# Storing a matmul's moving rows as pairs of 64-byte pieces in the expert stages and the feed-forward

## The chip, the cores and the metric

The kernel runs on one core of a Trainium2 chip, in one launch. The metric is device microseconds from start to end of the program; three runs of the kernel before gave 1620.09, 1614.03 and 1619.76 us, median 1619.76. Durations below come from one profiled execution of it, which took 1614.73 us, with a span of 1612.8 us from the first to the last recorded instruction.

## The reference, cut to what matters

Two transformer blocks on 256 tokens of width 1024, in fp32. The first ends in an expert layer (PEER), the second in a gated feed-forward with a short convolution:

```python
def peer_ffn(xn, wq, subkeys, u_tab, v_tab):          # T = 256 tokens, D = 1024
    q = (xt @ wq).reshape(T, 8, 2, 128)
    s = jnp.einsum('thpd,hpnd->thpn', q, subkeys)     # 8 heads x 2 halves x 128 keys
    ...                                               # top 16 of 128 x 128 = 16384 experts
    hdn = gelu(einsum('cd,chkd->chk', xc, u_tab[ic])) * gates
    return einsum('chk,chkd->cd', hdn, v_tab[ic])

    # second block, feed-forward (D_FF = 2816)
    u = conv_general_dilated(h @ w_up, w_conv, ...) + b_conv
    val, gt = jnp.split(u, 2, axis=-1)
    x = x + gate_f * ((jax.nn.silu(gt) * val) @ w_down)
```

## The kernel before, in words

Activations are held transposed: features on the 128 partitions, the 256 tokens along each partition. A row of 256 tokens in fp32 is 1024 bytes, and such a row is the *moving* operand of nearly every matmul; a 128x128 block of weights is the *stationary* one, loaded by a weight load (PEld) of its own while the matmul before it runs.

Precision comes from splitting. Each 128x1024 tile of weights is brought by one DMA of 512 KB (`raw`, L292), rounded by ScalarE into `hi` (L304), and VectorE forms `lo` = raw - hi (L306). The activations are split likewise into `xh` and `xl`, or `Hh` and `Hl` (`split`, L363 and L364). `mm3` then runs three matmuls per block, all of type fp32r with 256 columns: `hi` with `xh` (L322), `hi` with `xl` (L323), and after these `lo` with `xh` (L325). One tile of weights is 8 blocks, so 24 matmuls.

Three stages use it as the change touches it.

- The expert layer's first half (from 330 us to 782 us). `xh` and `xl` hold the normed input as eight rows. The queries are 16 units (`route`, `t_unit`), all but the first as `mm3`; then `u_pair` takes the 16384 rows of `u`, not gathered but all of them, as 128 units of 24 matmuls. Between them run the routing (VectorE, ScalarE) and, from 550 us on, the gates, which scale the result by the few experts chosen (`choose`, `gate`, with fp16 matmuls L1263).
- The expert layer's second half (782 to 1151 us). For each of 128 row blocks of `v`, one 256-token row of the hidden tile is split into `Hh` and `Hl`, and `mm3` adds it to eight accumulators `acc` in PSUM. After every second block `self.step()` advances a background job, `ada` (L376 to L399), by one step: it reads one more tile of modulation weights (`raw`, the same ring of 4 buffers) and VectorE multiplies and adds it (L388). After 8 such tiles 8 transposes follow (L394), and the next group begins.
- The feed-forward (1426 to 1607 us): 44 units of `up` with `xh`, `xl`; the first runs unsplit (L457), the second is split inside `norm_apply` (L465). Then 22 row blocks of `down` with `Hh`, `Hl`, interleaved two steps behind.

The instructions of an engine run in the order that they are queued. Weight tiles rotate through 4 `raw` buffers and, in the expert stages, 2 pairs of `hi` and `lo`. SyncE issues all DMAs in the order of the program.

`shim` places a tile: it allocates a few bytes in a pool and so shifts what follows. With `AT_U`, `AT_V` and `AT_FF` at 192, the rows of all three stages begin 192 bytes past a multiple of 256, and the weight blocks (512 bytes each) begin at a multiple of 256. The other stages (first mixer, second mixer) have the same form of matmul and are not touched.

Of the kernel before, what the change touches and what calls it, by code (L numbers as in the profile page):

```python
# [6 lines left out]
F32 = mybir.dt.float32  # L7
F32R = mybir.dt.float32r
# [8 lines left out]
T = 256  # L17
# [19 lines left out]

AT_B1, AT_U, AT_V, AT_B2, AT_FF = 192, 192, 192, 192, 192

# [230 lines left out]
class Prog:  # L270
# [17 lines left out]


    def raw(self, u, n=1024):  # L290
        t = self.wp.tile([128, 1024], F32, name="raw", tag="raw")
        self.sy.dma_start(t[:, :n], self.a["w"][u, :, :n])  # L292
        return t
# [19 lines left out]
    def mm3(self, terms, whi, wlo, xhi, xlo, inner=False):  # L313


        if inner:
            for t in terms:
                self.mm3([t], whi, wlo, xhi, xlo)
            return
        m = self.pe.matmul  # L320
        for out, w, x, start, stop in terms:
            m(out, whi[w], xhi[x], start=start, stop=False, skip_group_check=True)  # L322
            m(out, whi[w], xlo[x], start=False, stop=False, skip_group_check=True)  # L323
        for out, w, x, start, stop in terms:
            m(out, wlo[w], xhi[x], start=False, stop=stop, skip_group_check=True)  # L325

# [34 lines left out]

    def split(self, src, hi, lo):
        self.s.activation(hi, src, AF.Copy)  # L363
        self.v.tensor_tensor(lo, src, hi.bitcast(F32), OP.subtract)  # L364
# [78 lines left out]
    def norm_apply(self, h, gname, sh, sc, xh, xl, raws, pool, tag):  # L443
# [3 lines left out]
        ps = [pool.tile([128, T], F32, name="mmo", tag=tag, bufs=2) for _ in range(2)]  # L447
        for d in range(8):
# [4 lines left out]
            if whole:  # L453
                x = self.sm.tile([128, T], F32, name="nx", tag="sq", bufs=2)
                s.activation(x, tmp, AF.Identity, bias=sh[:, d:d + 1])
                for i in whole:
                    self.pe.matmul(ps[i], raws[i][:, c], x, start=(d == 0), stop=(d == 7))  # L457
                self.split(x, xh[:, d], xl[:, d])
            else:
                s.activation(xh[:, d], tmp, AF.Identity, bias=sh[:, d:d + 1])  # L460
                v.scalar_tensor_tensor(xl[:, d], tmp, sh[:, d:d + 1], xh[:, d].bitcast(F32), OP.add, OP.subtract)
            for p in range(3):
                for i in range(2):
                    if i not in whole:
                        self.pe.matmul(ps[i], raws[i][p // 2][:, c], (xh, xl, xh)[p][:, d], start=(d + p == 0), stop=(d == 7 and p == 2), skip_group_check=True)  # L465
        return ps
# [600 lines left out]
    def peer(self):  # L1067
# [25 lines left out]
        h = self.h  # L1093
        xh = xp.tile([128, 8, T], F32R, name="xh")
        xl = xp.tile([128, 8, T], F32R, name="xl")
        first = self.norm_apply(h, "n2", self.mod1[:, 24:32], self.mod1[:, 32:40], xh, xl, self.raws, ps2, "x")
        self.dump("xn2", xh.bitcast(F32))

# [224 lines left out]
        for i in range(128):  # L1323
            hi, lo = self.wsplit(wu["v"] + i)
            Hh = vp.tile([128, T], F32R, name="Hh")
            Hl = vp.tile([128, T], F32R, name="Hl")
            self.split(hslice(i // 2 * 2)[:, i % 2], Hh, Hl)
# [386 lines left out]
    def ffn(self):  # L1714
# [4 lines left out]
        with ExitStack() as st:  # L1719
# [6 lines left out]
            self.shim(rp, AT_FF)  # L1726
            xh = bp.tile([128, 8, T], F32R, name="xh")
            xl = bp.tile([128, 8, T], F32R, name="xl")
            self.shim(bp, 256 - AT_FF)
# [7 lines left out]
            def up(i):  # L1737
# [11 lines left out]
                v.tensor_tensor(val, val, gt, OP.mult)  # L1749
                Hh = rp.tile([128, T], F32R, name="Hh", tag="Hh")  # L1750
                Hl = rp.tile([128, T], F32R, name="Hl", tag="Hl")
                if i == 0:
# [34 lines left out]
```

## Time and profile before

| | |
|---|---|
| three runs | 1620.09, 1614.03, 1619.76 us |
| the profiled execution | 1614.73 us, span 1612.8 us |
| TensorE busy (matmul) | 1563.8 us, 97% of the span, 13022 matmuls |
| TensorE weight loads busy | 1500.2 us, 93% |
| VectorE, ScalarE busy | 1264.7 us (78%), 1020.4 us (63%) |
| granted TensorE clock, mean | 0.995 |
| DMA | 303.42 MB read, mean 190 GB/s |

A recorded matmul lasts from its start to its modelled end and overlaps the next, so a duration of 276 ns does not mean that one starts every 276 ns. The view of the chain that ended last gives the part of each that nothing overlaps: eight matmuls there with 0.91 us are spaced by 0.91 / 8 = 0.114 us.

### The profile page before, as it was taken

The page shows a single profiled execution, that of the slowest core. Times are in us where ns is not written, and L with a number is a line of the kernel's source. Part 1 is how long each engine was busy: PE and PEld are TensorE (multiplying, and loading weights), DVE is VectorE, ACT ScalarE, POOL GpSimd, SP SyncE. Part 2 cuts the span into 40 slices and gives each one's busy share as a digit, 9 for nine tenths or more (in the row PEclk, how much of TensorE's full clock was granted, in tenths as well). Part 3 has the DMA queues.
Part 4 walks back from the last instruction along what each step waited for, and adds up shares of the span by engine and source line. Part 5 has one row for each costly group of instructions (what it writes and reads, how often), then busy time and mean ns, then how long its engine had stood idle before and what let it go on. Part 6 is the DMA issues. An engine that isn't in the chain of part 4 may idle for free.

```text
span 1612.8 us, 33487 instructions
## 1 busy us (share of the span) xinstructions
PE 1563.8 (97%) x13022; PEld 1500.2 (93%) x13022; DVE 1264.7 (78%) x2731; ACT 1020.4 (63%) x2093; POOL 6.6 (0%) x43
## 2 busy tenths in 40 slices
PE   6999999999999999999999999999999999999998
PEld 5888898989999999999999999999898998889998
DVE  7887887878788787788777777777798886777776
ACT  4575765555545799998544444444678877755553
POOL 0000000000000000000000000000000000000000
PEclk8999999999999999999999999999999999999999
DMA  8632346645544544444677877788657322435553
GB/s 303 250 105 92 119 129 226 233 141 178 188 163 171 178 167 167 164 164 170 216 265 263 273 257 261 258 281 270 202 200 252 131 96 93 153 131 196 191 191 116
DMA packets 85262, 306.64 MB, mean 190 GB/s; under 512 B 9456, under 2 KB 10992, under 8 KB 84976
## 3 DMA queue, kind: packets, MB, share of 16 engines
q1 hardware_dynamic: 85104, 304.51, 55.5%
q8 instruction: 102, 1.67, 0.4%
q14 instruction: 56, 0.46, 0.1%
HBM read 303.42 MB, written 1.05 MB: 189 GB/s over the span
## 4 chain that ended last, share of the span: by engine, by line
PE 79%; DVE 9%; DMA 6%; ACT 3%; issue 1%; SPq 0%; DVEq 0%; ACTq 0%
PE mmo L322 14%; PE mmo L325 14%; PE mmo L323 13%; PE acc L323 6%; PE acc L322 6%; DMA raw<-w 6%; PE acc L325 5%; DVE lo L306 3%; PE pg L1263 2%; ACT hi L304 1%; PE facc L325 1%; PE facc L322 1%; PE facc L323 1%; PE z L699 1%; DVE acc L388 1%
## 5 line engine op out<-in xcount | busy, mean ns | idle before, releaser
L304 ACT ACTIVATE hi<-raw 128x1024 fp32r<-128x1024 f32 (+1 forms) x465 | 490.6, 1058 | 374.7 <-PE acc L323 167.7
L306 DVE TENSOR_TENSOR lo<-raw,hi 128x1024 fp32r<-128x1024 f32 (+1 forms) x465 | 565.5, 1218 | 171.9 <-ACT hi L304 168.1
L322 PE MATMUL mmo<-xh,hi 128*128 128x256 f32 x2032 | 496.8, 285 | 1.4 <-ACT hi L304 0.4
L323 PE MATMUL mmo<-xl,hi 128*128 128x256 f32 x2032 | 488.3, 280 | 0.0
L322 PEld LDWEIGHTS mmo<-xh,hi 128*128 128x128 f32 x2032 | 382.6, 189 | 5.4 <-ACT hi L304 1.7
L323 PEld LDWEIGHTS mmo<-xl,hi 128*128 128x128 f32 x2032 | 382.8, 188 | 2.0 <-issue 0.2
L325 PE MATMUL mmo<-xh,lo 128*128 128x256 f32 x2032 | 282.0, 280 | 4.7 <-DVE lo L306 4.6
L325 PEld LDWEIGHTS mmo<-xh,lo 128*128 128x128 f32 x2032 | 254.5, 188 | 7.1 <-DVE lo L306 6.5
L323 PE MATMUL acc<-Hl,hi 128*128 128x256 f32 x1024 | 244.6, 281 | 3.5 <-DVE Hl L364 2.6
L322 PE MATMUL acc<-Hh,hi 128*128 128x256 f32 x1024 | 243.7, 278 | 1.1 <-ACT Hh L363 1.1
L323 PEld LDWEIGHTS acc<-Hl,hi 128*128 128x128 f32 x1024 | 192.5, 188 | 8.0 <-DVE Hl L364 7.5
L322 PEld LDWEIGHTS acc<-Hh,hi 128*128 128x128 f32 x1024 | 192.4, 188 | 1.3 <-ACT Hh L363 1.3
L325 PE MATMUL acc<-Hh,lo 128*128 128x256 f32 x1024 | 139.5, 278 | 0.0
L325 PEld LDWEIGHTS acc<-Hh,lo 128*128 128x128 f32 x1024 | 127.3, 188 | 0.0
L388 DVE SCALAR_TENSOR_TENSOR acc<-raw,sil,acc 128x1024 f32<-128x1024 f32 x70 | 89.8, 1283 | 44.2 <-DMA raw<-w 43.9
L1245 ACT ACTIVATE D<-iota,i 128x128 f16<-128x128 f16 x256 | 84.6, 404 | 0.2
L1252 DVE TENSOR_TENSOR B<-O,iT 128x512 f16<-128x512 f16 x128 | 46.1, 418 | 0.0
L322 PE MATMUL facc<-Hh,hi 128*128 128x256 f32 x176 | 41.3, 276 | 0.0
L323 PE MATMUL facc<-Hl,hi 128*128 128x256 f32 x176 | 41.3, 276 | 0.0
L364 DVE TENSOR_TENSOR Hl<-hidA,Hh 128x256 fp32r<-128x256 f32 x96 | 40.2, 418 | 0.0
L363 ACT ACTIVATE Hh<-hidA 128x256 fp32r<-128x256 f32 x96 | 38.3, 400 | 0.0
L1246 ACT ACTIVATE A<-D 128x512 f16<-128x512 f16 x64 | 37.8, 628 | 0.0
(503 smaller groups left out, 2269.7 us busy)
## 6 DMA issues: line engine op xcount, KB each, us to landing
raw<-w SPq DMA_DIRECT2D x542, 512.0 KB, 4.2
aw<-w SPq DMA_DIRECT2D x16, 512.0 KB, 7.3
raw<-w SPq DMA_DIRECT2D x6, 384.0 KB, 3.5
whole<-w SPq DMA_DIRECT2D x4, 512.0 KB, 7.0
c<-w SPq DMA_DIRECT2D x3, 512.0 KB, 6.5
x<-xT SPq DMA_DIRECT2D x2, 512.0 KB, 5.8
hres<-xT SPq DMA_DIRECT2D x1, 1024.0 KB, 5.4
sk<-w SPq DMA_DIRECT2D x2, 512.0 KB, 5.5
```

The costliest lines, as they stand in the source:

```text
L304: self.s.activation(hi[:, :n], r[:, :n], AF.Copy)
L306: self.v.tensor_tensor(lo[:, :n], r[:, :n], hi[:, :n].bitcast(F32), OP.subtract)
L322: m(out, whi[w], xhi[x], start=start, stop=False, skip_group_check=True)
L323: m(out, whi[w], xlo[x], start=False, stop=False, skip_group_check=True)
L325: m(out, wlo[w], xhi[x], start=False, stop=stop, skip_group_check=True)
L363: self.s.activation(hi, src, AF.Copy)
L364: self.v.tensor_tensor(lo, src, hi.bitcast(F32), OP.subtract)
L388: v.scalar_tensor_tensor(acc, w, sc, acc, OP.mult, OP.add)
L1245: s.activation(D[:, j], iota, AF.Abs, bias=i1[:, t0 + j:t0 + j + 1])
L1246: s.activation(A, D, AF.Relu, scale=-1.0, bias=1.0)
L1252: v.tensor_tensor(B[p], O, row(1 + p), OP.mult)
L1263: mm(pg[:, j], B[p][:, :, j], A[:, j], start=(j + p == 0), stop=(j == 3 and p == 1), skip_group_check=True)
```

## The change

Each 256-token row of the moving operands in these three stages is stored in another order. It is seen as 16 pieces of 16 tokens (64 bytes). Even pieces go into the first 512 bytes of the row, odd pieces into the second 512: piece 2j lies at byte 64 j, piece 2j + 1 at byte 512 + 64 j. A matmul reads them in token order, so its moving access pattern goes 64 bytes in the lower half, 64 bytes in the upper half, and so on; outputs and sums are the same numbers in the same order. In the second half of the expert layer (`back=True`) the pairs are stored from the end, so that the addresses of the pairs fall while they are read.

`like` gives a plain row the matching view, so that the instructions that write `xh`, `xl`, `Hh`, `Hl` scatter, and PSUM is written as before. `AT_U` and `AT_V` go from 192 to 128, which moves the rows of both expert stages by 64 bytes.

Queues of SyncE and TensorE hold the same instructions in the same order. ScalarE's and VectorE's hold the same too, but the writers of these rows now have the form 128x8x2x16 in place of 128x256. On GpSimd the memsets of the shims change size, and one falls away.

```diff
-AT_B1, AT_U, AT_V, AT_B2, AT_FF = 192, 192, 192, 192, 192
+AT_B1, AT_U, AT_V, AT_B2, AT_FF = 192, 128, 128, 192, 192
...
+    def paired(self, pool, k, name, back=False, **kw):
+        t = pool.tile([128, k, 2, 8, 16], F32R, name=name, **kw)
+        if back:
+            t = t[:, :, :, ::-1]
+        return t.rearrange("p k e j w -> p k j e w")
+
+    def like(self, x, y):
+        return x.rearrange("p (j e w) -> p j e w", e=2, w=16) if len(y.shape) == 4 else x
...
         for out, w, x, start, stop in terms:
+            out = self.like(out, xhi[x])
             m(out, whi[w], xhi[x], start=start, stop=False, skip_group_check=True)
             m(out, whi[w], xlo[x], start=False, stop=False, skip_group_check=True)
         for out, w, x, start, stop in terms:
-            m(out, wlo[w], xhi[x], start=False, stop=stop, skip_group_check=True)
+            m(self.like(out, xhi[x]), wlo[w], xhi[x], start=False, stop=stop, skip_group_check=True)
...
     def split(self, src, hi, lo):
+        src = self.like(src, hi)
         self.s.activation(hi, src, AF.Copy)
...
-        xh = xp.tile([128, 8, T], F32R, name="xh")
-        xl = xp.tile([128, 8, T], F32R, name="xl")
+        xh, xl = self.paired(xp, 8, "xh"), self.paired(xp, 8, "xl")
...
-            Hh = vp.tile([128, T], F32R, name="Hh")
-            Hl = vp.tile([128, T], F32R, name="Hl")
+            Hh, Hl = self.paired(vp, 1, "Hh", True)[:, 0], self.paired(vp, 1, "Hl", True)[:, 0]
...
-            xh = bp.tile([128, 8, T], F32R, name="xh")
-            xl = bp.tile([128, 8, T], F32R, name="xl")
+            xh, xl = self.paired(bp, 8, "xh"), self.paired(bp, 8, "xl")
...
-                Hh = rp.tile([128, T], F32R, name="Hh", tag="Hh")
-                Hl = rp.tile([128, T], F32R, name="Hl", tag="Hl")
+                Hh, Hl = self.paired(rp, 1, "Hh", tag="Hh")[:, 0], self.paired(rp, 1, "Hl", tag="Hl")[:, 0]
```

## Rows read from the trace of the kernel before

**Rows 1.** The page's first part: busy time of each engine, share of the span, number of instructions.

```profile
PE 1563.8 (97%) x13022; PEld 1500.2 (93%) x13022; DVE 1264.7 (78%) x2731; ACT 1020.4 (63%) x2093; POOL 6.6 (0%) x43
```

**Rows 2.** Busy time by stage: first half of the expert layer in two parts, second half, feed-forward. Columns: stretch in us and its length; PE, PEld, DVE, ACT, POOL busy us (instructions); granted clock, DMA share, GB/s.

```profile
400.00:600.00 200.00, 195.98 (x1720) 193.28 (x1719) 162.92 (x426) 135.27 (x257) 0.00 (x0) 1.00 0.51 174
600.00:781.00 181.00, 181.00 (x1748) 179.88 (x1747) 151.46 (x300) 161.87 (x414) 0.25 (x2) 1.00 0.47 164
783.00:1151.00 368.00, 364.52 (x3121) 359.99 (x3121) 271.97 (x346) 174.61 (x255) 0.65 (x7) 1.00 0.79 264
1426.00:1607.00 181.00, 180.51 (x1570) 179.76 (x1570) 135.52 (x207) 104.25 (x162) 0.00 (x0) 1.00 0.50 169
```

**Rows 3.** The chain that ended last from 429 to 460 us (the `u` units): start us, us, engine, tile, line, count.

```profile
430.97 0.91 PE mmo L325 x8
433.69 0.91 PE mmo L325 x8
436.41 0.91 PE mmo L325 x8
439.13 0.91 PE mmo L325 x8
440.04 0.44 PE psc L1127 x4
...
443.03 0.94 PE mmo L325 x8
...
445.86 0.94 PE mmo L325 x8
...
448.69 0.94 PE mmo L325 x8
```

**Rows 4.** Matmuls by form (count | busy us, mean ns of one | idle before), in 442 to 457 us, then in 400 to 781 us, 783 to 1151 us and 1426 to 1607 us.

```profile
L325 PE MATMUL mmo<-xh,lo 128*128 128x256 f32 x40 | 5.5, 281 | 0.0
...
L323 PE MATMUL mmo<-xl,hi 128*128 128x256 f32 x971 | 231.2, 279 | 0.0
...
L325 PE MATMUL acc<-Hh,lo 128*128 128x256 f32 x1022 | 138.9, 278 | 0.0
...
L325 PE MATMUL mmo<-xh,lo 128*128 128x256 f32 x336 | 45.0, 276 | 0.0
```

**Rows 5.** Two forms with 128 fp32 columns moving against 128 columns of weights, by tile: count, duration ns min/median/max, first and last start.

```profile
L394 PE MATMUL mmo<-c,acc x80: 270/272/328, 220.8 to 1145.9; 128*128 128x128 f32 x80
...
L908 PE MATMUL pr<-V,MQ x32: 272/275/347, 146.9 to 276.2; 128*128 128x128 f32 x32
```

**Rows 6.** The transposes that end a group of the background job, in order of time: start us, us of the whole row; and from the view by tile the stage's first matmul: count, duration ns min/median/max, first and last start.

```profile
833.73 1.04 PE L394 MATMUL mmo<-c,acc 128*128 128x128 f32 x8
...
885.32 1.03 PE L394 MATMUL mmo<-c,acc 128*128 128x128 f32 x8
...
936.88 1.04 PE L394 MATMUL mmo<-c,acc 128*128 128x128 f32 x8
...
L322 PE MATMUL acc<-Hh,hi x1024: 276/276/384, 782.5 to 1151.3; 128*128 128x256 f32 x171
```

**Rows 7.** The chain by line from 783 to 1151 us, from 784 to 833 us and from 886 to 937 us, the first pieces of the last, and two rows of matmuls by form in 784 to 833 us and 835 to 885 us.

```profile
by line: PE acc L323 26.8%; PE acc L322 24.8%; PE acc L325 24.1%; DMA raw<-w 14.7%; DVE acc L388 2.9%; DVE lo L306 2.5%; issue 1.4%; ACT hi L304 1.4%; DVE Hl L364 1.0%; PE mmo L394 0.7%; DVEq L388 0.1%; DVEq L306 0.0%; ACTq L304 0.0%
...
by line: PE acc L323 33.9%; PE acc L322 33.4%; PE acc L325 32.9%
...
by line: DMA raw<-w 34.8%; PE acc L323 17.2%; PE acc L325 16.2%; PE acc L322 16.0%; DVE acc L388 7.8%; DVE lo L306 4.8%; issue 3.0%; DVE Hl L364 0.7%; DVEq L388 0.2%
...
886.96 4.01 DMA raw<-w
891.06 1.30 DVE acc L388
892.37 4.64 DMA raw<-w
897.10 1.29 DVE acc L388
898.42 4.43 DMA raw<-w
902.94 1.29 DVE acc L388
...
L325 PE MATMUL acc<-Hh,lo 128*128 128x256 f32 x138 | 19.2, 281 | 0.0
...
L325 PE MATMUL acc<-Hh,lo 128*128 128x256 f32 x142 | 19.1, 277 | 0.0
```

**Rows 8.** The chain from 400 to 600 us and from 600 to 781 us, by line.

```profile
by line: PE mmo L325 24.1%; PE mmo L322 23.9%; PE mmo L323 23.3%; DVE lo L306 7.4%; DVE res L1187 4.5%; PE pg L1263 3.5%; PE psc L1127 2.2%; issue 1.9%; DVE eq L1186 1.6%; ACT hi L304 1.1%; DVE eq L1184 1.0%; DVE mr L1112 0.8%; DVE ti L1111
...
by line: PE mmo L322 29.7%; PE mmo L323 28.8%; PE mmo L325 28.6%; PE pg L1263 12.6%; ACT hi L304 0.5%; issue 0.0%
```

**Rows 9.** The splits of one hidden row in the second half, by tile: count, duration ns min/median/max.

```profile
L363 ACT ACTIVATE Hh<-hidA x96: 395/400/405, 782.0 to 1053.3; 128x256 fp32r<-128x256 f32 x96
L364 DVE TENSOR_TENSOR Hl<-hidA,Hh x96: 415/418/421, 782.7 to 1055.6; 128x256 fp32r<-128x256 f32 x96
```

**Rows 10.** Unsplit fp32 matmuls of 256 columns: four in a row in order of time (start us, us), and another form by tile (duration ns min/median/max).

```profile
1255.79 1.03 PE L616 MATMUL rp<-x,c 128*128 128x256 f32 x4
...
L703 PE MATMUL z<-x,whole x64: 377/379/774, 24.3 to 68.0; 128*128 128x256 f32 x64
```

More of the change, by code (lines that the diff above doesn't have):

```diff
@@ L459, in norm_apply @@
             else:
+                tmp = self.like(tmp, xh[:, d])
                 s.activation(xh[:, d], tmp, AF.Identity, bias=sh[:, d:d + 1])
@@ L464, in norm_apply @@
                     if i not in whole:
-                        self.pe.matmul(ps[i], raws[i][p // 2][:, c], (xh, xl, xh)[p][:, d], start=(d + p == 0), stop=(d == 7 and p == 2), skip_group_check=True)
+                        self.pe.matmul(self.like(ps[i], xh[:, d]), raws[i][p // 2][:, c], (xh, xl, xh)[p][:, d], start=(d + p == 0), stop=(d == 7 and p == 2), skip_group_check=True)
         return ps
@@ L1093, in peer @@
         h = self.h
-        xh = xp.tile([128, 8, T], F32R, name="xh")
-        xl = xp.tile([128, 8, T], F32R, name="xl")
+        xh, xl = self.paired(xp, 8, "xh"), self.paired(xp, 8, "xl")
         first = self.norm_apply(h, "n2", self.mod1[:, 24:32], self.mod1[:, 32:40], xh, xl, self.raws, ps2, "x")
-        self.dump("xn2", xh.bitcast(F32))
         ts = up.tile([128, 2, 8, 2, 16], F32, name="ts")
```

## The prediction

> **What bounds the kernel now.** I read the page's busy times first. TensorE is busy 97% of the span and the next engine 78% [rows 1], so a change to the matmuls' pace is a change to the time wherever TensorE's own pace ends the chain. Then I cut the span by stage: the granted clock is 1.00 in all three stages that the change touches [rows 2], that is the 2.4 GHz level, so the clock has nothing to give back.
>
> The chain of waits then shows something that busy time hides. In the `u` units the last eight matmuls of a unit take 0.91 us, and units follow every 2.72 us, so one matmul starts every 2.72 / 24 = 113.3 ns. Then the four `psc` matmuls come between, and from there on the same units, of the same shape, take 0.94 us and follow every 2.83 us: 117.9 ns [rows 3]. Nothing in these stretches waits for another engine. So there are two paces, and an interruption can change from one to the other. The mean duration by form tells them apart: 281 ns at the slow pace, 276 ns at the fast one [rows 4]; a duration is the spacing plus some 163 ns (276 - 113). With 278 to 279 ns in between, about 0.6 of the matmuls in the first expert half run slow ((279 - 276) / 5), 0.4 in the second, none in the feed-forward [rows 4].
>
> A matmul with 128 fp32 columns moves 512 bytes past a weight load of 512 bytes. Its row reads 272 ns, or (1.04 - 0.272) / 7 = 110 ns of spacing, 109 by the duration rule; another form of the same size reads 275, 112 ns [rows 5, 6]. There the two reads run at the same pace. The fp32r matmul moves 1024 bytes past its weight load in nearly the same time, so its reads go twice as fast as the weights'. My reading is that the moving read and the next weight load hold each other up when they come near in address: never or once at equal pace (109, 112), once or more when one overtakes the other (113.3, 117.7). No row shows the cause; the paces are what the rows show.
>
> **The change part by part.** By the code 8064 matmuls read paired rows: queries 15 x 24 = 360, `u` 128 x 24 = 3072, `v` 3072, feed-forward 43 x 24 + 22 x 24 = 1560. In the new order each 128 bytes read advance the address by 64 in either half, so the moving address rises (or with `back` falls) at the weights' own pace. I expect the paces of equal reads, 109 to 112 ns.
>
> *First expert half, 3432 matmuls.* Mean now: 0.6 x 117.7 + 0.4 x 113.3 = 115.9 ns. At 109: 3432 x 6.9 = 23.8 us saved; at 112: 13.5 us. The trace has no fp32r matmul with such a pattern, so the ends are also 113.3 (8.9 us) above and, on the losing side, the second rival. I take 110.5, the middle of the two rows: 3432 x 5.4 = 18.5 us. From 600 us on the chain is TensorE to 99.7%, before that to 77% [rows 8], so of about half of it a quarter is lost to VectorE: 16.5 us.
>
> *Feed-forward, 1560 matmuls, all at 113.3 ns.* At 109: 6.7 us; at 112: 2.0; at 110.5: 4.4 us.
>
> *Second expert half, 3072 matmuls.* By the same count 3072 x (115.1 - 110.5) = 14 us would go, but here another chain is late next. One group of the background job is 18 blocks of experts and lasts from transposes to transposes: 885.32 - 833.73 = 51.6 us, then 936.88 - 885.32 = 51.6 [rows 6]. From 784 to 833 us every matmul runs slow (281 ns) and the chain is all TensorE [rows 7]; that group, too, took some 51 us (833.73 less the stage's start at 782.5 [rows 6]). From 835 us on nearly all run fast (277 ns), 18 x 24 x 4.4 ns = 1.9 us less per group, and yet the group lasts as long, because the chain goes through DMA for 35% of it: a tile lands after 4 to 4.6 us, VectorE adds it in 1.3 us, and only then its buffer takes the next, 5.8 to 6.0 us for two blocks of experts [rows 7] against 2 x 24 x 113.3 = 5.4 us of matmuls. VectorE waits there for the tile with the next `Hl` and `lo` queued behind it, and TensorE waits for those. A faster pace meets that same ring: 1 us of the 14 is my value, 0 to 8 the bounds.
>
> *Writers.* The splits of `Hh` and `Hl` (400 and 418 ns [rows 9]) keep their element count but scatter into 64-byte pieces. No row shows a scattered write of this type. Below, nothing changes; above, if they doubled, ScalarE and VectorE would gain 128 x 0.4 = 51 us each over 368 us in which they are busy 175 and 272 [rows 2]: with VectorE in the ring above it would cost up to 0.4 us per block. I take nothing: the elements and the order stay.
>
> *Shims and order.* GpSimd is busy 0% [rows 1]; nobody waits for the changed memsets. SyncE's and TensorE's queues are unchanged.
>
> Sum: 16.5 + 4.4 + 1 = 22 us from the profiled 1614.7, so 1592.7 us. The three runs lie between 1614 and 1620 with the profiled one at the low end, so for a median I say 1595.
>
> **A page against it.** Rows 3 show two paces with nothing waited for. The Trainium skill (SBUF — State Buffer, "Who interferes with whom") says that TensorE's moving operand and its weight loads have independent read ports and that TensorE never waits on anyone. By that rule the order of the pieces could not matter and the sum would be 0; two paces of one shape with one pair of operands speak against it, and the first rival keeps it alive.
>
> **The rivals.** *No change.* The two paces come from something other than the addresses (the phase in which TensorE restarts), and the paired rows fall into the same two. For: the pace changes after an interruption, not with the operands [rows 3]. Against: rows 5 show two paces at equal size too, both lower. Time 1614.7, in a median 1613 to 1620.
>
> *Only the slow pace goes.* 113.3 ns is fp32r's own floor, and paired rows only avoid the second hold-up. For: the feed-forward sits at 276 ns without one exception in its mean [rows 4]. Then 3432 x 0.6 x 4.4 = 9 us less the quarter, 8 us, and nothing in the feed-forward or behind the ring: 1606.
>
> *Slower: a price at each break.* A row now has 15 breaks between pieces. If one costs x ns, a matmul takes 109 + 15 x; with 115.9 and 113.3 now, it loses from x = 0.3 to 0.46 on. At 0.83 ns (two cycles at 2.4 GHz, the granted level) the pace is 121.5 ns: 3432 x 5.6 = 19 us, feed-forward 1560 x 8.2 = 13, and in the second half 432 x 121.5 = 52.5 us plus the transposes' 1 exceed the ring's 51.6 by 2 us in 7 groups, 14: about 46 us, 1660. For: no row has a matmul whose moving operand breaks. Its far end is a fall to the unsplit fp32 pace, (1.03 - 0.38) / 3 = 217 ns [rows 10], 8064 x 102 ns = 820 us. Against it speaks a rule of the Trainium skill (SBUF — State Buffer, the note on cachelines): only going to a new 16-byte line costs, and 64-byte pieces touch as many lines as before; by it the price is 0. No run here shows it.
>
> **How the numbers follow.** Forecast (paces of 109 to 112 ns): 0.55. Only the slow pace goes: 0.17. No change: 0.14. Slower: 0.14. The forecast's own range is 1614.7 - 13.5 x 0.88 - 2 = 1601 to 1614.7 - 23.8 x 0.88 - 6.7 - 8 = 1579, with up to 5 us above for a median. The range for 8 in 10 adds the two next cases, up to 1618, and at the low end a little for a second half that gains more than its bound: 1576. A measurement tells some 0.5%, 8 us, from no change. Faster by more: the forecast and most of the second case, 0.55 + 0.14 = 0.69. Within: 0.14 + 0.03 = 0.17. Slower: 0.14.
>
> **What would show it.** Durations by form: `mmo` L323 and `facc` L325 at 272 to 275 ns means the pace of equal reads; 276 throughout the second case; 276 and 281 mixed no change; above 281 a price at breaks. The groups of the second half at 51 us, with the DMA's share of its chain up from 15% [rows 7], would bear out the ring; at 48 to 49 us (18 x 24 x 110.5 + 1) the ring gave way and I am short by up to 14 us. `Hh` at 400 and `Hl` at 418 ns show that scattered writes are free. A median above 1618 or below 1576 makes the prediction wrong.

## The result: slower, and the profile after

The changed kernel took 1642.17 us (median of 4 runs, 1638.19 to 1644.93), the kernel before 1618.18 in the same session (4 runs, 1614.03 to 1620.09). The ratio is 1.0139, 95% interval 1.0107 to 1.0171: slower by 24 us, where 1595 had been forecast, with 0.14 for slower. The profiled execution after has a span of 1640.1 us against 1612.8.

First the page's busy times and the windows by stage of the kernel after (columns as in [rows 1] and [rows 2]; the stages now begin later, so the stretches are moved).

```profile
PE 1593.7 (97%) x13022; PEld 1531.9 (93%) x13022; DVE 1265.3 (77%) x2731; ACT 1021.8 (62%) x2093; POOL 6.6 (0%) x43
```

```profile
600.00:793.00 193.00, 193.00 (x1806) 191.59 (x1806) 156.88 (x311) 169.29 (x431) 0.00 (x0) 1.00 0.45 159
795.00:1166.00 371.00, 366.78 (x3120) 363.39 (x3121) 272.35 (x347) 174.96 (x257) 0.66 (x7) 1.00 0.78 262
1444.00:1634.00 190.00, 189.62 (x1563) 188.82 (x1562) 134.59 (x205) 103.71 (x160) 0.00 (x0) 1.00 0.47 161
```

The instruction counts are those of before, VectorE and ScalarE are as busy as before to 0.6 and 1.4 us, and only TensorE has more: 1593.7 against 1563.8 us. The clock is granted in full, so it is not the clock. TensorE's instructions take longer, and the chain says which. In the `u` units after (start us, us, what; compare [rows 3]):

```profile
442.63 0.96 PE mmo L337 x8
443.59 0.45 PE psc L1140 x4
...
446.57 0.96 PE mmo L337 x8
...
449.45 0.96 PE mmo L337 x8
...
452.33 0.96 PE mmo L337 x8
...
455.21 0.96 PE mmo L337 x8
```

Eight matmuls take 0.96 us and a unit follows every 2.88 us: 2.88 / 24 = 120.0 ns, before the `psc` matmuls and after them. The two paces of before, 113.3 and 117.7, are gone, and one pace slower than either stands in their place.

Where the 27.3 us between the two spans lie is read from the first and last start of two forms. After, then before (the view by tile: count, duration ns min/median/max, first and last start us):

```profile
L334 PE MATMUL acc<-Hh,hi x1024: 275/278/388, 795.4 to 1166.7; 128*128 128x256 f32 x171
...
L334 PE MATMUL facc<-Hh,hi x176: 282/283/284, 1462.0 to 1634.4; 128*128 128x256 f32 x176
```

```profile
L322 PE MATMUL facc<-Hh,hi x176: 276/276/276, 1444.2 to 1607.1; 128*128 128x256 f32 x176
```

The second half begins at 795.4 instead of 782.5 [rows 6], so all up to the end of the first half costs 12.9 us. The second half lasts 1166.7 - 795.4 = 371.3 instead of 1151.3 - 782.5 = 368.8 [rows 6]: 2.5 us. From its end to the first `facc` 295.3 instead of 292.9: 2.4 us, of which about 0.8 belong to the up matmuls of the feed-forward's first units; the rest is an unchanged stage. From the first to the last `facc` 172.4 instead of 162.9: 9.5 us. Together 27.3. (The medians differ by less, 24, because the profiled execution before, 1614.7 us, was a fast one of its kernel; see the last section.)

The forms in 600 to 793, 795 to 1166 and 1444 to 1634 us answer to [rows 4]: 282 and 283 ns in the stages read upward, 278 in the second half, whose rows are read from the end.

```profile
L337 PE MATMUL mmo<-xh,lo 128*128 128x256 f32 x464 | 65.1, 282 | 0.0
...
L337 PE MATMUL acc<-Hh,lo 128*128 128x256 f32 x1021 | 140.0, 278 | 0.0
...
L337 PE MATMUL facc<-Hh,lo 128*128 128x256 f32 x174 | 25.3, 283 | 0.0
```

The writers in the second half after, by tile (answering [rows 9]), the groups of the background job (the transposes in three stretches, answering [rows 6]), and the chain by line from 795 to 1166 us (answering [rows 7]):

```profile
L376 ACT ACTIVATE Hh<-hidA x96: 394/401/404, 795.0 to 1067.2; 128x256 fp32r<-128x256 f32 x96
L377 DVE TENSOR_TENSOR Hl<-hidA,Hh x96: 416/418/422, 795.7 to 1069.5; 128x256 fp32r<-128x256 f32 x96
```

```profile
L407 PE MATMUL mmo<-c,acc x8: 272/272/273, 847.1 to 847.9; 128*128 128x128 f32 x8
...
L407 PE MATMUL mmo<-c,acc x8: 272/272/273, 899.9 to 900.7; 128*128 128x128 f32 x8
...
L407 PE MATMUL mmo<-c,acc x8: 270/272/273, 951.0 to 951.7; 128*128 128x128 f32 x8
```

```profile
by line: PE acc L335 30.6%; PE acc L334 29.4%; PE acc L337 28.9%; DMA raw<-w 5.7%; PE mmo L407 1.4%; DVE lo L317 1.4%; DVE Hl L377 0.8%; DVE acc L401 0.7%; ACT hi L315 0.6%; issue 0.5%; ACT Hh L376 0.1%; DVEq L317 0.0%; ACTq L315 0.0%; DVEq
```

Scattered writing is free (401 and 418 ns). Two groups last 52.8 and 51.1 us, about the ring's 51.6, but the DMA's share of the chain fell from 14.7% to 5.7%: TensorE at 116.2 ns nearly fills the ring's time by itself (18 x 24 x 116.2 ns = 50.2 us, and 1 us of transposes).

### The profile page after: what moved, and what is told of

It reads as the page before. It is cut to its first block, busy times and chain, and to the rows that moved or that the text cites. A ratio compares the mean times of both kernels' runs of the same rounds, so it can differ in the third digit from the quotient of the medians.

```text
span 1640.1 us, 33488 instructions
## 1 busy us (share of the span) xinstructions
PE 1593.7 (97%) x13022; PEld 1531.9 (93%) x13022; DVE 1265.3 (77%) x2731; ACT 1021.8 (62%) x2093; POOL 6.6 (0%) x43
## 4 chain that ended last, share of the span: by engine, by line
PE 83%; DVE 8%; ACT 4%; DMA 4%; issue 1%; SPq 0%; DVEq 0%; ACTq 0%
PE mmo L334 14%; PE mmo L335 14%; PE mmo L337 14%; PE acc L335 7%; PE acc L334 7%; PE acc L337 7%; DMA raw<-w 3%; DVE lo L317 3%; PE pg L1276 2%; ACT hi L315 1%; PE facc L335 1%; PE facc L337 1%; PE facc L334 1%; PE pxt L907 1%; PE pz L895 1%
## 5 line engine op out<-in xcount | busy, mean ns | idle before, releaser
L334 PE MATMUL mmo<-xh,hi 128*128 128x256 f32 x2032 | 511.6, 289 | 1.0 <-ACT hi L315 0.4
L335 PE MATMUL mmo<-xl,hi 128*128 128x256 f32 x2032 | 503.3, 284 | 0.0
L337 PE MATMUL mmo<-xh,lo 128*128 128x256 f32 x2032 | 289.1, 283 | 3.1 <-DVE lo L317 2.7
L337 PEld LDWEIGHTS mmo<-xh,lo 128*128 128x128 f32 x2032 | 260.8, 189 | 5.5 <-DVE lo L317 4.7
```

The lines of the kernel that those rows point to most:

```text
L337: m(self.like(out, xhi[x]), wlo[w], xhi[x], start=False, stop=stop, skip_group_check=True)
```

## The experiments

Each kernel is the kernel after with the edit shown. "Pace" is the mean gap from one matmul's start to the next within a stage, gaps of 100 to 135 ns only, so that waits are left out. (Durations serve only roughly: a gap of 120.0 goes with 281 to 284 ns, as below.) The three lengths come from starts as above: I, the start of the second half; II, from the first to the last `acc<-Hh,hi`; III, from the first to the last `facc<-Hh,hi`. Layouts: "64 up 128" is pairs of 64-byte pieces read from the start at offset 128, "down" is read from the end, "plain" an unbroken row.

| kernel | first half: ns, I | second half: ns, II | feed-forward: ns, III | us |
|---|---|---|---|---|
| before | plain 192: 115.8, 782.5 | plain 192: 114.8, 368.8 | plain 192: 113.4, 162.9 | 1618.2 |
| after | 64 up 128: 120.1, 795.4 | 64 down 128: 116.2, 371.3 | 64 up 192: 120.0, 172.4 | 1642.2 |
| e1 | 64 up 0: 120.0, 797.3 | 64 down 0: 120.7, 380.3 | 64 up 0: 120.0, 172.5 | 1651.6 |
| e2 | 64 up 64: 120.0, 796.1 | 64 down 64: 116.7, 369.8 | 64 up 64: 120.0, 172.4 | 1641.3 |
| e3 | 64 up 192: 120.0, 797.7 | 64 down 192: 117.4, 372.7 | 64 up 128: 120.0, 172.5 | 1645.4 |
| e4 | 64 down 128: 116.3, 787.1 | 64 up 128: 120.8, 380.3 | 64 down 192: 117.4, 168.6 | 1638.1 |
| e7 | 64 up 160: 120.4, 794.5 | 64 down 160: 116.6, 371.0 | 64 up 160: 120.0, 172.5 | 1637.8 |
| e8 | 128 up 128: 120.0, 796.1 | 128 down 128: 119.0, 374.4 | 256 up 192: 113.4, 162.8 | 1635.3 |
| e9 | 256 up 192: 115.8, 783.5 | 256 up 192: 114.9, 369.6 | 64 up 192, 576 apart: 120.0, 172.5 | 1626.6 |
| e10 | plain 128: 118.7, 790.2 | plain 128: 119.1, 375.3 | one stretch, 64 down, 192: 117.8, 169.2 | 1635.8 |
| e11 | plain 64: 116.6, 785.9 | plain 64: 117.8, 376.2 | one stretch, 64 swapped, 192: 120.0, 172.4 | 1636.4 |
| e12 | plain 192: 115.8, 782.9 | 64 down 128: 116.6, 369.8 | plain 192: 117.7, 169.3 | 1621.4 |
| e13 | 256 up 128: 118.7, 791.0 | 256 up 64: 117.8, 373.6 | 32 up 192: 123.3, 177.2 | 1644.4 |
| e14 | 256 down 128: 118.7, 790.9 | 256 down 192: 115.9, 371.2 | halves swapped, 192: 113.4, 162.9 | 1626.8 |
| e15 | 256 up 0: 119.9, 793.4 | plain 0: 120.0, 376.9 | 256 up 64: 117.7, 169.2 | 1641.6 |
| e16 | plain 224: 118.4, 789.8 | plain 160: 118.3, 373.5 | plain 224: 118.3, 170.0 | 1635.1 |
| e17 | 256 up 192: 115.6, 783.6 | 256 up 192: 114.8, 369.2 | 256 up 192: 117.7, 169.2 | 1624.0 |

The times of before, after, e12 and e17 are medians of several executions, the others are of one; since executions of one kernel can differ by up to 14 us (last section), the argument goes by the paces and lengths of the stages, each read from one profiled execution. e5, e6 and e18 leave a part of the work out and stand further down. The kernel before, run beside each group of them, had medians of 1615.8 to 1621.4 us.

**Place and direction (e1 to e4).** My theory A was that of the prediction: the moving read and the next weight load hold each other up where addresses meet, so place and direction decide. Theory B was a fixed price at each break between pieces.

```diff
# e1; e2 has 64, 64, 64 and e3 192, 192, 128
-AT_B1, AT_U, AT_V, AT_B2, AT_FF = 192, 128, 128, 192, 192
+AT_B1, AT_U, AT_V, AT_B2, AT_FF = 192, 0, 0, 192, 0
```

```diff
# e4; the feed-forward's Hh, Hl as its xh, xl
-        xh, xl = self.paired(xp, 8, "xh"), self.paired(xp, 8, "xl")
+        xh, xl = self.paired(xp, 8, "xh", True), self.paired(xp, 8, "xl", True)
...
-            Hh, Hl = self.paired(vp, 1, "Hh", True)[:, 0], self.paired(vp, 1, "Hl", True)[:, 0]
+            Hh, Hl = self.paired(vp, 1, "Hh")[:, 0], self.paired(vp, 1, "Hl")[:, 0]
...
-            xh, xl = self.paired(bp, 8, "xh"), self.paired(bp, 8, "xl")
+            xh, xl = self.paired(bp, 8, "xh", True), self.paired(bp, 8, "xl", True)
```

> Paired rows as changed, but the rows of all three stages begin at a multiple of 256 bytes, where the weight blocks begin too. Theory A (the moving read and the next weight load hold each other up where their addresses meet): the pace depends on the place, so at least one stage leaves the changed kernel's pace of 120 ns (first expert half, feed-forward) or 115 to 117 ns (second half, read from the end) by 3 ns or more; at equal starts I expect the worst, 120 or more. Theory B (each break between pieces has a fixed price): 120 ns in the first half and the feed-forward whatever the place, the second half at 115 to 117; time within 5 us of the changed kernel's 1642.

> Paired rows 64 bytes past a multiple of 256 in all three stages. Theory A: the pace differs from that at 0 and at 128 or 192 by 3 ns or more in at least one of the two forward stages; at its best 109 to 113 ns, which over 3432 + 1560 matmuls is 33 to 55 us less than at 120. Theory B: 120 ns in the first half and the feed-forward, no difference.

> The places of the stages exchanged: 192 in both expert halves, 128 in the feed-forward. Theory A: the first half takes the pace that the feed-forward had at 192 and the reverse; since both were 120 ns, both stay at 120; the second half, read from the end, may leave its 115 to 117 ns by 3 ns or more. Theory B: 120, 120 and 115 to 117 ns, no difference.

> The direction turned at the changed kernel's places: first half and feed-forward read from the end, second half from the start. Theory A: direction decides, so the first half and the feed-forward fall to 113 to 117 ns and the second half rises to 120; the first half alone then saves 3432 x 3 to 7 ns = 10 to 24 us. Theory B: direction is no part of a price at breaks: 120 ns stays in the first half and the feed-forward; that the second half runs at 115 to 117 would then be its waits or its other form (one row in place of eight).

The second half at 0 (e1), and the second half and feed-forward turned round (e4), by tile:

```profile
L334 PE MATMUL acc<-Hh,hi x1024: 278/283/389, 797.3 to 1177.6; 128*128 128x256 f32 x171
```

```profile
L334 PE MATMUL acc<-Hh,hi x1024: 279/282/386, 787.1 to 1167.4; 128*128 128x256 f32 x171
...
L334 PE MATMUL facc<-Hh,hi x176: 277/280/282, 1461.9 to 1630.5; 128*128 128x256 f32 x176
```

Read upward, 64-byte pairs take 120.0 ns at 0, 64, 128 and 192 in the first half and the feed-forward, and 120.8 in the second half at 128 (e4). That is against A. Read from the end they take 116.2 at 128, 116.7 at 64, 117.4 at 192 and 120.7 at 0, which is against a plain B. Neither survived as put. At 120.8 ns the second half takes 380.3 us: there the ring no longer sets the end.

**The weight load made narrow (e5, e6, e18).** If the moving read waits for the weight load beside it, a load of a quarter of the columns must change the pace. The edit leaves the lo part out for output rows 32 to 127, so the matmul writes a quarter of its output rows too.

```diff
-            m(self.like(out, xhi[x]), wlo[w], xhi[x], start=False, stop=stop, skip_group_check=True)
+            m(self.like(out, xhi[x])[0:32], wlo[w][:, 0:32], xhi[x], start=False, stop=stop, skip_group_check=True)
```

e5 has the layout of after and took 1646.6 us, e6 has plain rows at 192 (1610.8 us); e18 has plain rows at 0 and at 128 in the expert stages and 32-byte pieces in the feed-forward (1642.3 us).

> The kernel after, in which the lo*x matmuls of the three stages use only 32 of their 128 weight columns (so the lo part reaches output rows 0 to 31 alone and is left out for the other 96; rows read, pieces and order are those of after). The 8 (or 2) lo matmuls of a group then run beside weight loads of 32 columns, while hi matmuls still run beside full ones; the pace is read at the gaps between lo matmuls, of which the kernel after has all at 120.0 ns in the first half and the feed-forward. Theory A, in the form that the first four runs leave (the moving read is held up by the weight load beside it, in a way that the direction of reading decides): lo matmuls fall to 113.3 ns or less, hi ones stay at 120.0; total about 1630 us. Theory B (a price of the pieces themselves, paid by the moving read alone): lo matmuls stay at 120.0 in both stages, total 1642.

> The same edit (lo*x with 32 of 128 weight columns, the lo part left out for output rows 32 to 127), with plain rows at offset 192 in the three stages, as the kernel before has them (113.3 and 117.7 ns in two regimes). Theory A: beside narrow loads a plain row is read at one pace of its own, 109 to 112 ns, and the gaps of 117.7 are gone among lo matmuls while they remain among hi ones. Theory B in its rest (the weight load takes no part): lo gaps as hi gaps, 113.3 and 117.7 mixed; total within 0.3% of 1618 in that case, 1600 to 1610 by A.

> The lo*x matmuls of the three stages use 32 of 128 weight columns again (the lo part left out for output rows 32 to 127). First half: plain rows at 0; second half: plain rows at 128; feed-forward: paired rows with 32-byte pieces at 192. Full weight loads gave 119.9 ns at 0, 119.1 at 128 and 123.3 for the 32-byte pieces. Theory A for plain rows (the place acts through the weight load beside the row): the gaps between lo matmuls fall to 113.3 in both expert stages. Theory B for short pieces (their price is the moving read's own): 123.3 stays in the feed-forward. If the place acts on the moving read by itself, the gaps between lo matmuls stay at 119.9 and 119.1.

By tile, e5 (second half hi and lo, feed-forward lo), then e18 (the same); by form in 600 to 781 us, e6; and two weight loads of e6, full and narrow, 188 and 108 ns:

```profile
L334 PE MATMUL acc<-Hh,hi x1024: 275/278/383, 796.1 to 1169.7; 128*128 128x256 f32 x171
L337 PE MATMUL acc<-Hh,lo x1024: 277/283/284, 798.4 to 1169.9; 128*32 128x256 f32 x171
...
L337 PE MATMUL facc<-Hh,lo x176: 283/283/284, 1468.5 to 1639.3; 128*32 128x256 f32 x176
```

```profile
L336 PE MATMUL acc<-Hh,hi x1024: 274/281/387, 790.6 to 1163.0; 128*128 128x256 f32 x171
L339 PE MATMUL acc<-Hh,lo x1024: 274/276/285, 792.9 to 1163.2; 128*32 128x256 f32 x171
...
L339 PE MATMUL facc<-Hh,lo x176: 284/286/288, 1459.4 to 1635.0; 128*32 128x256 f32 x176
```

```profile
L337 PE MATMUL mmo<-xl,hi 128*128 128x256 f32 x444 | 104.5, 277 | 0.0
L339 PE MATMUL mmo<-xh,lo 128*32 128x256 f32 x448 | 60.1, 276 | 0.0
```

```profile
L336 PEld LDWEIGHTS acc<-Hh,hi x1024: 186/188/333, 777.6 to 1148.4; 128*128 128x128 f32 x171
...
L339 PEld LDWEIGHTS acc<-Hh,lo x1024: 107/108/170, 779.8 to 1148.7; 128*32 128x32 f32 x171
```

e5: beside narrow loads the lo matmuls of the two upward stages keep 120.0 ns, so the size of the weight load takes no part in that pace. In e18 the 123.3 ns of the 32-byte pieces stay too. Rows read from the end are another matter: the lo matmuls of e5's second half went up, from 116.0 to 119.9 ns, when the loads beside them became smaller, which I had not expected and cannot explain.

Plain rows behave as A says, in part. In e6 gaps near 117.7 nearly vanish (means 113.8 for lo, 114.2 for hi, against 115.8 before) and the first half ends 4.9 us earlier (777.6 against 782.5). In e18 the lo gaps fall from 119.9 to 117.7 at 0 and from 119.1 to 114.8 at 128, not to the 113.3 that I had expected. So the slow pace of plain rows gives way, in part, when the lo matmuls are made narrow. That the load does it is not shown: the output is narrower too, and in e6 the hi matmuls, with full loads, became faster as well. How much is left to the place alone is open. The second half gained nothing from 113.9 ns (370.9 us): the ring's limit held.

**How long a piece must be (e8, e13, e14, e7).**

```diff
# e8: width=32 in both expert stages, 64 in the feed-forward; e13: 64, 64 and 8
-    def paired(self, pool, k, name, back=False, **kw):
-        t = pool.tile([128, k, 2, 8, 16], F32R, name=name, **kw)
+    def paired(self, pool, k, name, back=False, width=16, **kw):
+        t = pool.tile([128, k, 2, 128 // width, width], F32R, name=name, **kw)
...
# e14's feed-forward (width 128) and, with width 16, e11's
+        if kind == "swap":
+            return pool.tile([128, k, T // (2 * width), 2, width], F32R, name=name, **kw)[:, :, :, ::-1]
...
# e7
-AT_B1, AT_U, AT_V, AT_B2, AT_FF = 192, 128, 128, 192, 192
+AT_B1, AT_U, AT_V, AT_B2, AT_FF = 192, 160, 160, 192, 160
```

> The kernel after with all three stages' paired rows at 160, an odd multiple of 32 bytes, so that every 64-byte piece of the rows straddles a multiple of 64 (directions as in after: first half and feed-forward from the start, second half from the end). If a line of 64 bytes is what a piece should stay inside (a form of theory B: a fetch per 64-byte line touched), a straddling piece costs two fetches and the forward stages go above 120.0, to 127 ns (16 more fetches at the 0.44 ns each that 15 breaks would have cost above 113.3), total about 1675. Theory A (direction and the weight load decide, as places in multiples of 64 did nothing): 120.0 forward, 116 to 118 backward, total 1642.

> The kernel after with longer pieces: 128 bytes in the first half (7 breaks, forward) and in the second (7 breaks, from the end), 256 bytes in the feed-forward (3 breaks, forward); places as in after. Theory B (a price at each break): from 113.3 with no break to 120.0 with 15, so 116.5 ns in the first half and 114.7 in the feed-forward, total about 1620. Theory A (the two halves' 512 bytes of distance and the direction decide, length plays no part): 120.0 in both, total 1642.

> Feed-forward: paired rows with pieces of 32 bytes (31 breaks) at 192, forward. First half: 256-byte pieces, forward, at 128; second half: 256-byte pieces, forward, at 64. Theory B1 (a row out of rising order in short pieces is read in another way, which costs 6.7 ns once, however many breaks): feed-forward 120.0 ns. Theory B2 (each break costs, and something hides the first few: none visible at 3, 6.7 ns at 7 and at 15): more than 120, about 126. Expert stages: rows of 256-byte pieces were as plain ones at 192; if they are read as plain ones, they take the paces of plain rows at these places too: first half at 128 about 118.7 ns and 456 us, second half at 64 about 117.8 and 376. If long pieces free a row from its place, 113.3 to 116 and 440 to 449 us in the first half.

> Feed-forward: one stretch of 1024 bytes at 192 whose two halves of 512 bytes stand swapped (one break). First half: 256-byte pieces from the end at 128; second half: the same at 192. Theories B1 and B2 alike: one break of long pieces is not seen, feed-forward 113.3 (or in the second regime of plain rows, 117.7, as in the run of the second half alone). Expert stages: read from the end, short pieces took 116.2 (at 128) and 117.4 (at 192); if the direction matters for long pieces too, so here, else as for rows read upward at these places.

e8's feed-forward by tile and its first half in the chain (unit after unit 2.88 us), then the feed-forward of e13 and of e14:

```profile
L336 PE MATMUL facc<-Hh,hi x176: 276/276/276, 1464.8 to 1627.6; 128*128 128x256 f32 x176
```

```profile
450.60 0.96 PE mmo L339 x8
453.48 0.96 PE mmo L339 x8
456.36 0.96 PE mmo L339 x8
```

```profile
L334 PE MATMUL facc<-Hh,hi x176: 284/288/288, 1459.7 to 1636.9; 128*128 128x256 f32 x176
```

```profile
L336 PE MATMUL facc<-Hh,hi x176: 276/276/276, 1456.3 to 1619.2; 128*128 128x256 f32 x176
```

In the feed-forward at 192 the pace is 113.4 ns with 1 break (512-byte pieces) and 3 (256 bytes), 120.0 with 15 (64 bytes) and 123.3 with 31 (32 bytes); e13's 123.3 lies between what the two forms of theory B had expected, 120.0 and about 126. Pieces of 128 bytes (7 breaks, read upward) ran only in the first half, at 128: 120.0 ns, where 256-byte pieces take 118.7, and 796.1 us to its end against 791.0 (e8, e13). So there is a price, and it is neither one per row nor one per break. At 256 bytes none is seen, at 128 bytes there is one; its size at 192 was not measured. Pieces that straddle a multiple of 64 bytes (e7) cost nothing more.

**Distance and order (e9, e10, e11).**

```diff
# e9, the feed-forward's rows: halves 512 + 64 bytes apart
+        if kind == "far":
+            t = pool.tile([128, k, 320], F32R, name=name, **kw)[:, :, :2 * (128 + FAR)]
+            t = t.rearrange("p k (e r) -> p k e r", e=2)[:, :, :, :128].rearrange("p k e (j w) -> p k e j w", w=width)
...
# e10, the feed-forward's rows
+        if kind == "rev":
+            return pool.tile([128, k, T // width, width], F32R, name=name, **kw)[:, :, ::-1]
...
# e9's expert stages: width=64 at 192; e10's and e11's: plain rows at 128 and at 64
```

> Feed-forward: paired rows as in after (64-byte pieces, from the start, at 192), but the second half begins 576 bytes behind the first instead of 512. Both expert stages: paired rows with 256-byte pieces read from the start, at 192. Theory A (own pace of a paired row: two pieces 512 bytes apart stand in each other's way, as long as a piece is 128 bytes or less; the weight load takes no part): the feed-forward falls from 120.0 to 113.3 ns (span of its down matmuls 172.7 to 163.1 us). Theory B (any row whose pieces of 128 bytes or less are not in rising order costs 120, at any distance): it stays at 120.0. For the expert stages both say what the eighth run showed in the feed-forward: 113.3 to 113.4, unless the second regime of plain rows (117.7) comes up there too: first half 440 to 448 us. Total 1612 by A, 1622 by B.

> Feed-forward: rows in one stretch of 1024 bytes at 192, no halves, but written and read in 64-byte pieces from the end to the start (each piece rising inside). Both expert stages: plain rows at 128 instead of 192. Theory A (two halves 512 bytes apart): neighbours here lie 64 bytes apart, so 113.3 ns in the feed-forward. Theory B (any order of short pieces that does not rise costs): 120.0 or more there (15 breaks, all backward). Expert stages: if the regimes of a plain row (113.3, 117.7) depend on where the row stands, as the pace of rows read from the end did (116.2 at 128, 117.4 at 192, 120.7 at 0), the first half leaves its 448.5 us by 5 or more; if not, it stays within 3 of it.

> Feed-forward: rows in one stretch of 1024 bytes at 192, 64-byte pieces with each pair of neighbours swapped (second piece read first), so 15 breaks of 64 or 192 bytes and no two pieces 512 apart in a row. Both expert stages: plain rows at 64. Theory A (512 bytes of distance): 113.3 ns in the feed-forward; theory B (order): 120.0. Expert stages as in the run before: place matters if the first half leaves 448.5 us by 5 or more.

The feed-forward by tile in e9, e10 and e11:

```profile
L341 PE MATMUL facc<-Hh,hi x176: 282/283/284, 1446.4 to 1618.9; 128*128 128x256 f32 x176
```

```profile
L340 PE MATMUL facc<-Hh,hi x176: 279/281/282, 1459.0 to 1628.2; 128*128 128x256 f32 x176
```

```profile
L338 PE MATMUL facc<-Hh,hi x176: 283/284/285, 1456.6 to 1629.0; 128*128 128x256 f32 x176
```

A wider distance leaves 120.0, and neighbours swapped inside one stretch, no two of them 512 bytes apart in succession, take 120.0 too. So the 512 bytes are not the cause: short pieces out of order are. Short pieces in rising order, with gaps between them, were not tried, so the breaks are not separated from the order. One stretch read from the end takes 117.8, like the other rows read down.

**Places for plain and long-piece rows (e15, e16, and the expert stages of e10, e11, e13).**

```diff
# e15: width=64 in the first half and the feed-forward, plain in the second half
-AT_B1, AT_U, AT_V, AT_B2, AT_FF = 192, 128, 128, 192, 192
+AT_B1, AT_U, AT_V, AT_B2, AT_FF = 192, 0, 0, 192, 64
# e16: plain rows in all three
+AT_B1, AT_U, AT_V, AT_B2, AT_FF = 192, 224, 160, 192, 224
```

> First half: 256-byte pieces forward at 0; second half: plain rows at 0; feed-forward: 256-byte pieces forward at 64. Theory A for rows read as plain ones (the weights begin at 0 modulo 256, and the row's place against them decides how much the two reads interfere): at 0 the interference is largest, 120 or more in both expert stages, and 116 to 118 in the feed-forward. Rival: place is not what decides, and both stages stay at the paces of 192 (115 to 116, feed-forward 113.4).

> Plain rows in all three stages, at 224 in the first half and the feed-forward and at 160 in the second half (odd multiples of 32 bytes). So far plain rows took 119.9 ns at 0, 116.6 to 117.8 at 64, 118.7 to 119.1 at 128 and 113.3 or 117.7 at 192. If the interference of the row with the weight load follows the place smoothly, 224 lies between 192 and 256 (that is, 0): 115 to 119 ns, first half 449 to 458 us; 160 lies between 128 and 192: 115 to 119. Rival: a place that is no multiple of 64 is out of step with the weights and free of it, 113.3 in both: first half 440 us, total about 1604.

```profile
L336 PE MATMUL acc<-Hh,hi x1024: 278/283/387, 793.4 to 1170.3; 128*128 128x256 f32 x171
...
L336 PE MATMUL facc<-Hh,hi x176: 279/279/280, 1464.8 to 1634.0; 128*128 128x256 f32 x176
```

```profile
L336 PE MATMUL facc<-Hh,hi x176: 277/280/286, 1457.5 to 1627.5; 128*128 128x256 f32 x176
```

(First e15, then e16.) With the weights at multiples of 256, plain rows take 120.0 ns at 0, 116.6 to 117.8 at 64, 118.3 at 160, 118.7 to 119.1 at 128, 118.3 to 118.4 at 224, and 113.3 or 117.7 at 192, the place of before. Rows of 256-byte pieces read upward have about the pace of plain ones at each place tried. None of these six places is free of the slow pace, and no version with all its work beats the kernel before.

**The whole undone in two ways, timed (e12, e17).** e12 keeps the change in the second half alone; e17 keeps all of it but with 256-byte pieces, upward, at 192.

```diff
# e12
-        xh, xl = self.paired(xp, 8, "xh"), self.paired(xp, 8, "xl")
+        xh, xl = self.paired(xp, 8, "xh", kind="plain"), self.paired(xp, 8, "xl", kind="plain")
...
# e17
-        xh, xl = self.paired(xp, 8, "xh"), self.paired(xp, 8, "xl")
+        xh, xl = self.paired(xp, 8, "xh", width=64), self.paired(xp, 8, "xl", width=64)
```

> The change in the second half alone: first half and feed-forward with plain rows at 192, as before; second half paired, from the end, at 128, as after. Both theories give the stage its cost in the two traces: second half 371.5 us against 369.1, first half and feed-forward as before; total 1616 to 1622, same within 0.5%. Were the stages not additive (a longer first half, for one, giving time back in the second, which waits on its weights), it would come out 5 or more above.

> The kernel after with pieces of 256 bytes instead of 64, read from the start, and at the places of before (192) in all three stages; halves still 512 bytes apart and read pair by pair. If the short pieces alone cost the 24 us (theory B), all of them are gone: paces of plain rows (115.8, 114.9 and 113.4 or 117.7 ns), total as before within 0.5%, 1614 to 1628. If pairs as such cost something as well (theory A in what was left of it: two places read in turn), the feed-forward or the first half stays above its pace before by 1 ns or more, total 1623 or more in the mean.

e12: 1621.44 us, ratio to before 1.0001, interval 0.9976 to 1.0025. e17: 1624.01 us, ratio 1.0006, 0.9986 to 1.0026. So the first half and the feed-forward carry the loss. With 256-byte pieces at 192, halves, pairs and scattered writes show no cost beyond the interval, 0.3%. But e17 undoes three things at once: the length of the pieces, the move of the expert rows from 192 to 128, and the direction in the second half. Other rows tell them apart: 64-byte pairs at 192 (e3), plain rows at 128 (e10), 256-byte pieces at 128 and 64 (e13) and at 192 (e17); the first start is the end of the first half.

```profile
L334 PE MATMUL acc<-Hh,hi x1024: 276/280/388, 797.7 to 1170.4; 128*128 128x256 f32 x171
```

```profile
L340 PE MATMUL acc<-Hh,hi x1024: 274/282/387, 790.2 to 1165.5; 128*128 128x256 f32 x171
```

```profile
L334 PE MATMUL acc<-Hh,hi x1024: 276/279/384, 791.0 to 1164.6; 128*128 128x256 f32 x171
```

```profile
L334 PE MATMUL acc<-Hh,hi x1024: 276/276/384, 783.6 to 1152.8; 128*128 128x256 f32 x171
```

In the feed-forward the place stayed at 192, and the length alone decides: 113.4 or 117.7 ns with 256 bytes, 120.0 with 64. In the first half the move to 128 costs plain rows 7.7 us (790.2 against 782.5), and 64-byte pieces cost 15.2 us at 192 (797.7) and 12.9 at 128 (795.4). Each is a loss by itself, they do not add up, and moving the short pieces back would have saved nothing. In the second half, at 128, the pairs read from the end are faster than plain rows (116.2 against 119.1 ns, 371.3 against 375.3 us).

## Why the prediction was wrong, by its own steps

*What bounds the kernel* held. TensorE's own pace ends the chain in the first half and the feed-forward, and the lengths follow the pace: with the forecast's own rule (a quarter lost before 600 us, 0.88 in all) 3432 x (120.0 - 115.8) x 0.88 = 12.7 us, measured 12.9; feed-forward 1560 x (120.0 - 113.4) = 10.3, measured 9.5 and some 0.8 ahead of the first `facc`. Only the change of the pace had the wrong sign.

*The step that failed* is the one in "the change part by part" that takes the paired rows to the paces of equal reads, 109 to 112 ns, because their addresses rise at the weights' pace. It needed two things. One is that the moving read and the weight load hold each other up. For plain rows e6 and e18 fit that, though they do not separate the load from the output. By the Trainium skill (SBUF — State Buffer, "Who interferes with whom") the two read ports are independent and TensorE never waits. The fall from 119.1 to 114.8 ns in e18, where load and output are narrower, and the 120.0 ns that plain rows take in the second half at 0 (e15) against 114.8 at 192, speak against it but do not settle it. The other is that a broken row, left alone, is read as fast as an unbroken one. That was not in any row, and it is false: 120.0 ns at every place, with a full load beside it (e1 to e3) or one of a quarter of the columns (e5, at 128 and 192). The argument took the pace of one operand order for a property of the pair of reads, and left out of its sum what the new order costs by itself.

*A term put at nothing without a reason* is the other half of the edit, the move of the expert rows from 192 to 128. For plain rows it takes the first half from 115.8 to 118.7 ns and costs 7.7 us (e10). The result does not show it, because rows of short pieces take 120 ns at either place (e3), but with 256-byte pieces it would have shown (e13: 791.0 against 782.5 us).

*"113.3 ns is fp32r's own floor"*, the case with 0.17, is nearer the truth for plain rows: nothing went below 113.3 for long in any of the three stages of any run, even beside narrow loads (e6). So the 109 ns of [rows 5] did not carry over to a row of twice the bytes, and the most that ridding the first half of its slow pace could give is 3432 x 2.5 x 0.88 = 7.6 us.

*The slower rival* had the right kind of cause and nearly the right pace, 121.5 ns against 120.0, but a wrong form: not 0.83 ns at each of 15 breaks (e8, e13, e14). It counted from 109 ns, which no stage of any run came to, so the nearness of its pace is in part luck. Its 1660 is 18 us too much, mostly from the second half, where it put 14 us. There the rows are read from the end and take 116.2 ns, 3072 x 1.4 = 4 us more matmul time, of which the ring hid a part: 2.5 us. Read upward the same stage costs 11.5 (e4), so the rival's count of the ring was sound. The rule that spoke against this rival, the Trainium skill's note on 16-byte cachelines (SBUF — State Buffer), makes the price of 64-byte pieces 0. The traces do not agree: at the same place the feed-forward takes 120.0 ns with 64-byte pieces, 113.4 or 117.7 with 256-byte ones (e8, e17).

*Ring, writers, shims* held: groups of 51 to 53 us, no gain in the second half from a faster pace (e6), 401 and 418 ns for the scattered splits. The DMA's share of the chain fell where the prediction had it rise, because the pace rose. A small reading was off: [rows 7] give 5.4, 6.0 and 5.8 us for two blocks, not 5.8 to 6.0, with the same mean as 51.6 / 9 = 5.7.

*Open.* Why pieces of 128 bytes and less cost and those of 256 do not; why rows read from the end vary with the place and go slower beside a smaller weight load; whether it is the load by which the place of a plain row acts, and what is left of the place without it.

## What to carry to other kernels

Before an operand is stored in another order, measure the new order's pace by itself; a stage with narrow weight loads beside it shows whether their size takes part. For this matmul rows cut into pieces of 256 bytes or more kept the pace of an unbroken row at the same place; pieces of 64 bytes read upward took 120 ns everywhere, more than the slow pace (117.7) that they were to remove. A row's place is to be measured too: 64 bytes lower, an unbroken row took 118.7 ns in place of 115.8. Where the pace is all that changes, count it stage by stage: the stages that end in TensorE pay in full, the one behind a ring pays what sticks out.

## What the runs showed that I had not expected

One layout can run at two paces for a whole stage: the feed-forward with plain rows at 192 took 162.9 us in the trace before and 169.3 in e12's, each constant from start to end, and 256-byte pieces 162.8 (e8) and 169.2 (e17). The rows of the two that took longer:

```profile
L336 PE MATMUL facc<-Hh,hi x176: 281/281/281, 1445.1 to 1614.4; 128*128 128x256 f32 x176
```

```profile
L334 PE MATMUL facc<-Hh,hi x176: 281/281/281, 1447.6 to 1616.8; 128*128 128x256 f32 x176
```

(e12, then e17.) These are different kernels with the same feed-forward; that two executions of one kernel differ so is not shown, as each was profiled once. If they do, these 6.4 us make up nearly half of the 14 us by which 13 runs of the kernel before differ (1614.08 to 1628.22). The profiled 1614.7, with its feed-forward at 276 ns throughout [rows 4], is near the lowest of them, and the prediction's "none in the feed-forward" was read from that one execution. Short pieces read upward have no such second pace: 172.4 or 172.5 us in all seven kernels that have them in the feed-forward.
